# More buffers for the last stage of a one-layer hybrid encoder: eight row tiles, four raw weight tiles, another order in the first MLP chunk

## The chip, the cores and the metric

The kernel runs on one core of one Trainium2 chip. A core has a matrix engine (TensorE, PE in the profile, with its weight loads shown apart as PEld), a vector engine (VectorE, DVE), a scalar engine (ScalarE, ACT), a general engine (GpSimd, POOL), and an engine that here only issues transfers (SyncE, SP). Each engine works through its own instructions in a fixed order and waits on semaphores for the others. The on-chip memory SBUF has 128 partitions; the matrix engine adds up its products in PSUM. The metric is the device time of one execution in microseconds (us), the median of several runs.

## The reference, cut to what matters

The program computes one step of a layer on 2048 prompt rows and 32 sample rows, each 1024 wide, in float32:

```python
qa, ka, va, qb, kb, vb = split_proj(rmsnorm(hp, g_attn), w_in)
oa = diff_attn_prompt(qa, ka, va, t5_table, lam)      # group A
ob = band_attn_prompt(qb, kb, vb, band_table)         # group B
hp = hp + merge(oa, ob, subln_g, out_norm_b, w_out, lam_init)   # concat @ w_out
# ffn_ple:
c = rmsnorm(h, g_mlp)
h = h + jnp.square(jax.nn.relu(c @ w_up)) @ w_down    # 1024 -> 4096 -> 1024
h = h + jax.nn.sigmoid(h @ w_ple_gate) * (p @ w_ple_proj)
y = rmsnorm(h, g_final)
```

The attention outputs are normalised, joined and projected by w_out; then come the MLP, the gate and the final norm. The attention takes most of the program's text and is not touched.

## The kernel before, in words

**Blocks.** The 2080 rows are four blocks of columns (the data lie transposed, features on the partitions): blocks 0 to 2 have 512 columns, block 3 has 544 and is multiplied as two halves of 272. A row of 128 features of one block is one small tile, 128 x 512 or 128 x 544.

**Three products for one.** Every operand is split into a high part, which the matrix engine takes at full speed, and a low part, the rest. `mm3` (L186 to L192) issues hi x hi (L190), hi x lo (L191) and lo x hi (L192) for each of the terms; 24 matmuls make one product of 1024 terms. `split` makes the parts: the high part on ACT (L169), the low part on POOL in pieces of 256 columns at most (L164 for weights, L154 for rows) or on DVE (L175).

**Weights.** `wunit` (L177) brings one unit of 512 KB: a load into a raw tile `wr`, of which there are two, then wh on ACT and wl in four pieces on POOL; wh and wl have three tiles each. A raw tile is free once both parts have been made.

**Small tiles.** One ring of four tiles with the tag "tmp" is shared by five users: `raw_o` loads a row of the attention output (oraw), `outproj` loads the residual row it adds to (hd) and keeps its square (tmp), `cnorm` loads a row of h to be normalised (tmp), and `mlp_up` keeps the relu of a product (relu).

**Order.** The program is written as Python generators that are woven by hand; a list scheduler of the framework then fixes, before the run, the order of each engine's instructions from its own model of durations and of which tiles are free. So the number of tiles changes not only what must wait but also the order. All transfers are issued by SP (L145) in one order: a load whose tile isn't free holds up all those behind it. Where a pool of tiles is opened over the space of an older one, a new tile waits until the old one that lies there was last read.

**The last stage** begins where the pools wk4, fk4, md, acth and hh are opened (about L1225). Blocks 0 and 1 have been through the MLP by then, and gate(1) and final(1) are just ending. What follows:

- `outproj(2)`: for each of eight output rows d, one weight unit, 24 matmuls, the sum with hd on DVE (L860), the square on ACT, its sum on POOL (sqacc), and the store of hd to hS. It is woven with `oload(3)`, which loads the eight rows k of block 3's attention output (oraw), scales four of them (L835, DVE) and splits them (oact).
- `outproj(3)`, the same for block 3, 48 matmuls of 272 columns for each d.
- `gate(0)`: eight weight units of w_ple_gate; the low and high parts of h are hL and hH; sigmoid and sums are sig and sm on ACT, POOL and DVE (L1015 to L1034), and the result goes into h on POOL.
- `cnorm(2)` and `cnorm(3)`: for each of eight rows a load of tmp from hS, a scaling (L881, DVE), and the split into cH (ACT) and cL (POOL for even rows, DVE for odd ones). The parts of block 3 lie where gate(0) has hH and hL, so they wait for its last matmul.
- `final(0)`: transposes (yp), the final norm (yn) and the stores to y_prompt.
- `mlp` on blocks 2 and 3: 16 chunks of two weight units f0, f1; in each, `mlp_up` makes the products (ups) of both units with both blocks, relu, square (L936, L937) and the split into uh and ul; `mlp_down` of the chunk before adds its products (dps) to h (L971, DVE).
- gate(2), gate(3) and their finals end the program.

In `mlp_up` the loop over f stands outside, the loop over the blocks inside; the first products are f0 x block 2, f0 x block 3, f1 x block 2, f1 x block 3.

Of the kernel before, what the change touches and what calls it, by code (L numbers as in the profile page):

```python
# [12 lines left out]
F32 = mybir.dt.float32  # L13
F32R = mybir.dt.float32r
AF = mybir.ActivationFunctionType
# [4 lines left out]
P = 128  # L20
# [13 lines left out]
BLK = 544  # L34
SUBS = {
    0: [(0, 512)],
    1: [(0, 512)],
    2: [(0, 512)],
    3: [(0, 272), (272, 272)],
}  # L40
# [67 lines left out]
class Rings:  # L108
    def __init__(self, *rings):
        self.rings, self.i = rings, 0  # L110
# [23 lines left out]
class Kern:  # L134
    def __init__(self, tc, a):
        self.tc = tc
        self.nc = tc.nc
        self.a = a

    def dma(self, dst, src):  # L140
        if dst.dtype == F32R:
            dst = dst.bitcast(F32)
        if src.dtype == F32R:
            src = src.bitcast(F32)
        self.nc.sync.dma_start(dst, src)  # L145
# [30 lines left out]

    def wunit(self, src, shape, hi_eng="act", lo_eng="pool"):  # L177
        nc = self.nc
        raw = self.wp.tile([P] + shape, F32, tag="wr", bufs=2, name="wr")
        self.dma(raw, src)  # L180
        hi = self.wp.tile([P] + shape, F32R, tag="wh", bufs=3, name="wh")
        lo = self.wp.tile([P] + shape, F32R, tag="wl", bufs=3, name="wl")
        self.split(hi, lo, raw, hi_eng, lo_eng)
        return hi, lo
# [615 lines left out]
                self.dma(self.pS[:, 1, k, t0 : t0 + n], lo[:, :n])  # L800

    def raw_o(self, wk, k, t0, n):
        t = wk.tile([P, BLK], F32, tag="tmp", bufs=4, name="oraw")[:, :n]
        self.dma(t, self.oT[:, k, t0 : t0 + n])
        return t

# [34 lines left out]
    def outproj(self, b, wk, oact, ps, acc):  # L841
        nc, a = self.nc, self.a
        n, t0 = BN[b], 512 * b
        W = a["w_out"][0]
        sq = wk.tile([P, BLK], F32, tag="acc", bufs=2, name="sqacc2")[:, :n]
        acc.append(sq)
        for d in range(8):
            wh, wl = self.wunit(W[:, P * d : P * d + P].rearrange("(k p) c -> p k c", p=P), [8, P])
            h = wk.tile([P, BLK], F32, tag="tmp", bufs=4, name="hd")[:, :n]
            self.dma(h, self.xT[:, d, t0 : t0 + n])  # L850
            for s0, sn in SUBS[b]:
                p = ps.tile([P, 512], F32, tag="mm", name="ops")[:, :sn]
                self.mm3(
                    p,
                    [
                        (wh[:, k], wl[:, k], oact[0][k][:, s0 : s0 + sn], oact[1][k][:, s0 : s0 + sn])
                        for k in range(8)
                    ],
                )
                nc.vector.tensor_tensor(h[:, s0 : s0 + sn], h[:, s0 : s0 + sn], p, op=ALU.add)  # L860
            if d == 0:
                nc.scalar.activation(sq, h, AF.Square)
            else:
                tmp = wk.tile([P, BLK], F32, tag="tmp", bufs=4, name="tmp")[:, :n]
                nc.scalar.activation(tmp, h, AF.Square)
                self.pool_tt(sq, sq, tmp, ALU.add)
            self.dma(self.hS[:, d, t0 : t0 + n], h)
            yield

    def cnorm(self, b, wk, act, out):  # L870
        nc = self.nc
        n, t0 = BN[b], 512 * b
        cH = act.tile([P, 8, act.aw], F32R, tag="act", name="cH")
        cL = act.tile([P, 8, act.aw], F32R, tag="act", name="cL")
        out[b] = (cH, cL)
        r = wk.tile([P, BLK], F32, tag="r", bufs=2, name="rl")[:, :n]
        self.dma(r, self.rS[:, t0 : t0 + n])
        for k in range(8):
            tmp = wk.tile([P, BLK], F32, tag="tmp", bufs=4, name="tmp")[:, :n]
            self.dma(tmp, self.hS[:, k, t0 : t0 + n])  # L880
            nc.vector.scalar_tensor_tensor(  # L881
                tmp, tmp, self.g_mlp[:, k : k + 1], r, op0=ALU.mult, op1=ALU.mult
            )
            self.split(cH[:, k, :n], cL[:, k, :n], tmp, "act", "dve" if k % 2 else "pool")
            yield
# [31 lines left out]
    def mlp_up(self, ch, nf, blocks, st, wk, up, mm):  # L917
        nc = self.nc
        Wu = self.a["w_up"][0]
        us = {}  # L920
        for f in range(nf):
            ft = nf * ch + f
            wh, wl = self.wunit(Wu[:, P * ft : P * ft + P].rearrange("(k p) c -> p k c", p=P), [8, P])
            for b in blocks:
                h, cH, cL = st[b]
                uh = up.tile([P, up.aw], F32R, tag="u", name="uh")
                ul = up.tile([P, up.aw], F32R, tag="u", name="ul")
                us[f, b] = (uh, ul)
                for s0, sn in SUBS[b]:
                    ps = mm.tile([P, 512], F32, tag="mm", name="ups")[:, :sn]  # L930
                    self.mm3(
                        ps,
                        [(wh[:, k], wl[:, k], cH[:, k, s0 : s0 + sn], cL[:, k, s0 : s0 + sn]) for k in range(8)],
                    )
                    r = wk.tile([P, BLK], F32, tag="tmp", bufs=4, name="relu")[:, :sn]
                    nc.scalar.activation(r, ps, AF.Relu)  # L936
                    nc.scalar.activation(r, r, AF.Square)  # L937
                    self.split(uh[:, s0 : s0 + sn], ul[:, s0 : s0 + sn], r, "act", "pool")
        return us

    def mlp_down(self, ch, nf, blocks, us, st, wk, mm):
# [154 lines left out]
    def run(self):  # L1096
        tc, nc, a = self.tc, self.nc, self.a
        with ExitStack() as top:

            def opened(stack, name, bufs, space=None, side="left"):  # L1100
                kw = {} if space is None else {"space": space}
                return stack.enter_context(
                    tc.tile_pool(name=name, bufs=bufs, side=side, reuse_waits="tile", **kw)
                )
# [2 lines left out]
            cp = opened(top, "cp", 1)  # L1107
            self.dp = opened(top, "dp", 1, bass.MemoryType.DRAM)
            self.wp = opened(top, "wp", 3)
            mm = opened(top, "mm", MM, PSUM)  # L1110
            tp = mm
            psx = ExitStack()
# [16 lines left out]
            with ExitStack() as x:  # L1129
                wk = opened(x, "setup", 1, side="right")  # L1130
# [5 lines left out]
            with ExitStack() as x:  # L1136
                pool = opened(x, "a0", 1, side="right")
# [42 lines left out]
            with ExitStack() as x:  # L1180
                pool = opened(x, "a1", 1, side="right")
                for js in JA1:
                    self.attn_a(js, pool, ps_s, ps_t, ps_o)
            wk = opened(sq_, "wk", 1)
            fk = opened(sq_, "fk", 1)
            self.gfin(fk)
            acc, cn, st = {}, {}, {}
# [12 lines left out]
            up = Sized(opened(top, "uh", 16, side="right"), BLK)  # L1200
# [3 lines left out]
            def hload(pool, w, b):  # L1204
                h = pool.tile([P, 8, w], F32, tag="h", name="h")
                self.dma(h[:, :, : BN[b]], self.hS[:, :, 512 * b : 512 * b + BN[b]])
                return h

            for b in HALVES[0]:
# [4 lines left out]
                h = hload(hq, 512, b)  # L1214
# [10 lines left out]
            psx.close()  # L1225
            wk = opened(top, "wk4", 1)
            fk = opened(top, "fk4", 1)
            self.gfin(fk)
            md = opened(top, "md", 8 - MM, PSUM, "right")
            act = Sized(opened(top, "acth", 4), BLK, True)  # L1230
# [6 lines left out]
            h = hload(hh, BLK, 0)  # L1237
# [6 lines left out]
            f = self.final(0, h, up, fk, mm)  # L1244
            st = {b: (hload(hh, BLK, b),) + cn[b] for b in HALVES[1]}
# [6 lines left out]
            f = self.final(2, st[2][0], up, fk, mm)  # L1252
# [4 lines left out]
            f = self.final(3, st[3][0], up, fk, mm, md)  # L1257
# [48 lines left out]
```

## Time and profile before

| what | us |
|---|---|
| median of three runs | 3277.6 (3271.13 to 3279.51) |
| profiled execution, its own time | 3282.74 |
| its span, first to last instruction | 3281.0 |
| PE busy in the span | 3096.6 |
| the last stage's beginning, 2180 to 2460: PE busy | 250.61 of 280 |
| the long MLP, 2460 to 3200: PE busy | 740.00 of 740 |
| the end, 3200 to 3281: PE busy | 67.17 of 81 |

The mean granted clock of PE in the profile is 0.974 of full speed. A row of the timeline gives the start, the duration of the group, the engine, the line, the operation, output and inputs with their shapes, the number of instructions, and in brackets the idle time ahead of it and what ended it. A row of the waits gives the engine and line that waited, the one that it waited for, the total, the number of times and the longest. In a chain of waits each piece is what the next one was waiting for. PE's matmuls overlap: the distance of two starts, not the duration shown, is what one costs.

### The profile page before, as it was taken

The page shows a single profiled execution, that of the slowest core. Times are in us where ns is not written, and L with a number is a line of the kernel's source. Part 1 is how long each engine was busy: PE and PEld are TensorE (multiplying, and loading weights), DVE is VectorE, ACT ScalarE, POOL GpSimd, SP SyncE. Part 2 cuts the span into 40 slices and gives each one's busy share as a digit, 9 for nine tenths or more (in the row PEclk, how much of TensorE's full clock was granted, in tenths as well). Part 3 has the DMA queues.
Part 4 walks back from the last instruction along what each step waited for, and adds up shares of the span by engine and source line. Part 5 has one row for each costly group of instructions (what it writes and reads, how often), then busy time and mean ns, then how long its engine had stood idle before and what let it go on. Part 6 is the DMA issues. An engine that isn't in the chain of part 4 may idle for free.

```text
span 3281.0 us, 51609 instructions
## 1 busy us (share of the span) xinstructions
PE 3096.6 (94%) x17881; PEld 2713.4 (83%) x17881; DVE 1562.2 (48%) x3952; ACT 1696.1 (52%) x3717; POOL 1711.0 (52%) x2515
## 2 busy tenths in 40 slices
PE   6998999899989999999999999998989999999998
PEld 6877788899877888778788877877779999999988
DVE  5116786444455544566655655735442232223235
ACT  4226676666656766666665656744442222222245
POOL 5436776433335544656654644676954333333377
PEclk9998999999999999999999999999989999999999
DMA  7488886876778654545655355357531111111123
GB/s 230 169 258 241 226 246 199 230 225 199 221 210 240 166 140 120 159 137 152 195 136 142 109 139 139 111 159 227 164 102 49 46 46 50 45 48 46 46 91 106
DMA packets 519085, 489.03 MB, mean 149 GB/s; under 512 B 37884, under 2 KB 414016, under 8 KB 518824
## 3 DMA queue, kind: packets, MB, share of 16 engines
q1 hardware_dynamic: 518824, 485.73, 50.8%
q8 instruction: 142, 2.33, 0.3%
q14 instruction: 119, 0.97, 0.1%
HBM read 379.06 MB, written 110.49 MB: 149 GB/s over the span
## 4 chain that ended last, share of the span: by engine, by line
PE 54%; DMA 5%; DVE 4%; POOL 2%; ACT 1%; issue 1%; SPq 0%; DVEq 0%; POOLq 0%; ACTq 0%
PE dps L190 7%; PE ups L191 7%; PE ups L190 7%; PE ups L192 7%; PE dps L192 7%; PE dps L191 7%; PE s L567 2%; PE gps L190 1%; PE gps L191 1%; DMA ka<-kS 1%; PE gps L192 1%; PE tpp L639 1%; POOL wl L164 1%; DMA wr<-w_up 1%; PE ob L766 1%
## 5 line engine op out<-in xcount | busy, mean ns | idle before, releaser
L164 POOL TENSOR_TENSOR wl<-wr,wh 128x256 fp32r<-128x256 f32 x936 | 690.9, 770 | 501.1 <-ACT wh L169 473.0
L971 DVE TENSOR_TENSOR h<-h,dps 128x512 f32<-128x512 f32 (+1 forms) x640 | 373.1, 585 | 597.5 <-PE dps L192 584.9
L169 ACT ACTIVATE wh<-wr 128x1024 fp32r<-128x1024 f32 x338 | 356.9, 1056 | 581.0 <-PE dps L191 285.7
L154 POOL TENSOR_TENSOR wl<-wr,wh 128x256 fp32r<-128x256 f32 x416 | 305.0, 764 | 407.0 <-ACT wh L169 403.7
L190 PE MATMUL dps<-uh,wh 128*128 128x512 f32 (+1 forms) x1280 | 458.6, 358 | 10.1 <-DVE h L971 5.5
L190 PE MATMUL ups<-cH,wh 128*128 128x512 f32 (+1 forms) x1280 | 453.3, 354 | 9.9 <-ACT relu L936 5.0
L191 PE MATMUL ups<-cL,wh 128*128 128x512 f32 (+1 forms) x1280 | 452.9, 354 | 4.1 <-DVE cL L175 3.6
L192 PE MATMUL ups<-cH,wl 128*128 128x512 f32 (+1 forms) x1280 | 453.2, 354 | 0.0
L191 PE MATMUL dps<-ul,wh 128*128 128x512 f32 (+1 forms) x1280 | 451.0, 353 | 0.0
L192 PE MATMUL dps<-uh,wl 128*128 128x512 f32 (+1 forms) x1280 | 450.9, 353 | 0.0
L154 POOL TENSOR_TENSOR ul<-relu,uh 128x136 fp32r<-128x136 f32 (+1 forms) x320 | 201.7, 652 | 167.7 <-ACT uh L169 166.4
L190 PEld LDWEIGHTS ups<-cH,wh 128*128 128x128 f32 x1280 | 242.8, 190 | 42.3 <-ACT relu L936 5.3
L190 PEld LDWEIGHTS dps<-uh,wh 128*128 128x128 f32 x1280 | 242.5, 189 | 42.4 <-DVE h L971 9.0
L191 PEld LDWEIGHTS ups<-cL,wh 128*128 128x128 f32 x1280 | 243.3, 190 | 36.0 <-DVE cL L175 3.8
L192 PEld LDWEIGHTS dps<-uh,wl 128*128 128x128 f32 x1280 | 242.0, 189 | 33.7
L192 PEld LDWEIGHTS ups<-cH,wl 128*128 128x128 f32 x1280 | 243.1, 190 | 30.1
L191 PEld LDWEIGHTS dps<-ul,wh 128*128 128x128 f32 x1280 | 242.2, 189 | 26.2
L190 PE MATMUL qps<-aH,wh 128*128 128x512 f32 (+1 forms) x640 | 231.3, 361 | 8.6 <-ACT kr L432 3.4
L191 PE MATMUL qps<-aL,wh 128*128 128x512 f32 (+1 forms) x640 | 229.6, 359 | 0.0
L192 PE MATMUL qps<-aH,wl 128*128 128x512 f32 (+1 forms) x640 | 228.9, 358 | 0.0
L567 PE MATMUL s<-ka,q 128*128 128x256 f32 (+4 forms) x784 | 190.4, 347 | 26.6 <-DMA ka<-kS 10.9
L581 ACT ACTIVATE e<-s,nm 128x512 f32<-128x512 f32 (+3 forms) x256 | 155.1, 611 | 68.7 <-DVE nm L573 46.0
(218 smaller groups left out, 7118.3 us busy)
## 6 DMA issues: line engine op xcount, KB each, us to landing
wr<-w_up SPq DMA_DIRECT2D x96, 512.0 KB, 4.2
wr<-w_down SPq DMA_DIRECT2D x96, 512.0 KB, 3.7
wr<-w_in SPq DMA_DIRECT2D x74, 512.0 KB, 5.2
q<-qS SPq DMA_DIRECT2D x256, 128.0 KB, 4.2
v<-vSa SPq DMA_DIRECT2D x64, 512.0 KB, 4.0
ka<-kS SPq DMA_DIRECT2D x32, 512.0 KB, 7.7
wr<-w_out SPq DMA_DIRECT2D x32, 512.0 KB, 5.4
wr<-w_ple_gate SPq DMA_DIRECT2D x32, 512.0 KB, 4.3
```

Of the source, the lines that this page charges most:

```text
L154: nc.gpsimd.tensor_tensor(out[:, sl], a[:, sl], b[:, sl], op=op)
L164: nc.gpsimd.tensor_tensor(out[:, sl], a[:, sl], b[:, sl], op=op)
L169: nc.scalar.activation(hi, raw, AF.Copy)
L190: nc.tensor.matmul(ps, lh, rh, start=start and i == 0, stop=False)
L191: nc.tensor.matmul(ps, lh, rl, start=False, stop=False)
L192: nc.tensor.matmul(ps, ll, rh, start=False, stop=stop and i == n - 1)
L567: nc.tensor.matmul(s, q[:, m, hl, P * qi : P * qi + nr], kt[:, m, k0 : k0 + n], start=hl == 0, stop=hl == 1)
L581: nc.scalar.activation(dst, src, AF.Exp, bias=nmx, accum_out=z[:nr, m, bi : bi + 1])
L639: nc.tensor.transpose(tp[:kn, x, :nr], w[:nr, P * i : P * i + kn], self.ident[:nr, :nr])
L766: nc.tensor.matmul(o[:, qa:qb], vt, pt[:kn, i - kfirst, qa:qb], start=x == 0 and y == 0, stop=x == len(order) - 1 and y == 1,)
L971: nc.vector.tensor_tensor(hv, hv, ps, op=ALU.add)
```

## The change: two rings made larger, one loop turned for one chunk, less scratch

- From the last stage on the ring "tmp" has eight tiles and not four (`self.nt`), for all its five users.
- From there on raw weight tiles come in turn from the old ring of two and from a new ring of two in the pool wk4 (`Rings`, a class that is in the kernel already, takes the next ring at each call).
- In the first chunk of each MLP the order of the products is all weight units for one block, then all for the next. It differs from the old order only where there are two blocks, in the last stage. Both weight units of the chunk are then used before block 3 is.
- The scratch that is set aside for descriptors is 1024 bytes. The added tiles need, in each partition, 4 x 544 x 4 = 8704 bytes and 2 x 4096 = 8192 bytes.

No operation is added or removed, and no byte is moved more.

```diff
--- before.py
+++ after.py
@@ -136,6 +136,7 @@
         self.tc = tc
         self.nc = tc.nc
         self.a = a
+        self.nt = 4
 
     def dma(self, dst, src):
         if dst.dtype == F32R:
@@ -176,7 +177,7 @@
 
     def wunit(self, src, shape, hi_eng="act", lo_eng="pool"):
         nc = self.nc
-        raw = self.wp.tile([P] + shape, F32, tag="wr", bufs=2, name="wr")
+        raw = self.rawp.tile([P] + shape, F32, bufs=2, name="wr")
         self.dma(raw, src)
         hi = self.wp.tile([P] + shape, F32R, tag="wh", bufs=3, name="wh")
         lo = self.wp.tile([P] + shape, F32R, tag="wl", bufs=3, name="wl")
@@ -800,7 +801,7 @@
                 self.dma(self.pS[:, 1, k, t0 : t0 + n], lo[:, :n])
 
     def raw_o(self, wk, k, t0, n):
-        t = wk.tile([P, BLK], F32, tag="tmp", bufs=4, name="oraw")[:, :n]
+        t = wk.tile([P, BLK], F32, tag="tmp", bufs=self.nt, name="oraw")[:, :n]
         self.dma(t, self.oT[:, k, t0 : t0 + n])
         return t
 
@@ -846,7 +847,7 @@
         acc.append(sq)
         for d in range(8):
             wh, wl = self.wunit(W[:, P * d : P * d + P].rearrange("(k p) c -> p k c", p=P), [8, P])
-            h = wk.tile([P, BLK], F32, tag="tmp", bufs=4, name="hd")[:, :n]
+            h = wk.tile([P, BLK], F32, tag="tmp", bufs=self.nt, name="hd")[:, :n]
             self.dma(h, self.xT[:, d, t0 : t0 + n])
             for s0, sn in SUBS[b]:
                 p = ps.tile([P, 512], F32, tag="mm", name="ops")[:, :sn]
@@ -861,7 +862,7 @@
             if d == 0:
                 nc.scalar.activation(sq, h, AF.Square)
             else:
-                tmp = wk.tile([P, BLK], F32, tag="tmp", bufs=4, name="tmp")[:, :n]
+                tmp = wk.tile([P, BLK], F32, tag="tmp", bufs=self.nt, name="tmp")[:, :n]
                 nc.scalar.activation(tmp, h, AF.Square)
                 self.pool_tt(sq, sq, tmp, ALU.add)
             self.dma(self.hS[:, d, t0 : t0 + n], h)
@@ -876,7 +877,7 @@
         r = wk.tile([P, BLK], F32, tag="r", bufs=2, name="rl")[:, :n]
         self.dma(r, self.rS[:, t0 : t0 + n])
         for k in range(8):
-            tmp = wk.tile([P, BLK], F32, tag="tmp", bufs=4, name="tmp")[:, :n]
+            tmp = wk.tile([P, BLK], F32, tag="tmp", bufs=self.nt, name="tmp")[:, :n]
             self.dma(tmp, self.hS[:, k, t0 : t0 + n])
             nc.vector.scalar_tensor_tensor(
                 tmp, tmp, self.g_mlp[:, k : k + 1], r, op0=ALU.mult, op1=ALU.mult
@@ -917,25 +918,29 @@
     def mlp_up(self, ch, nf, blocks, st, wk, up, mm):
         nc = self.nc
         Wu = self.a["w_up"][0]
-        us = {}
-        for f in range(nf):
+        us, w = {}, {}
+        order = [(f, b) for f in range(nf) for b in blocks]
+        if ch == 0:
+            order = [(f, b) for b in blocks for f in range(nf)]
+        for f, b in order:
             ft = nf * ch + f
-            wh, wl = self.wunit(Wu[:, P * ft : P * ft + P].rearrange("(k p) c -> p k c", p=P), [8, P])
-            for b in blocks:
-                h, cH, cL = st[b]
-                uh = up.tile([P, up.aw], F32R, tag="u", name="uh")
-                ul = up.tile([P, up.aw], F32R, tag="u", name="ul")
-                us[f, b] = (uh, ul)
-                for s0, sn in SUBS[b]:
-                    ps = mm.tile([P, 512], F32, tag="mm", name="ups")[:, :sn]
-                    self.mm3(
-                        ps,
-                        [(wh[:, k], wl[:, k], cH[:, k, s0 : s0 + sn], cL[:, k, s0 : s0 + sn]) for k in range(8)],
-                    )
-                    r = wk.tile([P, BLK], F32, tag="tmp", bufs=4, name="relu")[:, :sn]
-                    nc.scalar.activation(r, ps, AF.Relu)
-                    nc.scalar.activation(r, r, AF.Square)
-                    self.split(uh[:, s0 : s0 + sn], ul[:, s0 : s0 + sn], r, "act", "pool")
+            if f not in w:
+                w[f] = self.wunit(Wu[:, P * ft : P * ft + P].rearrange("(k p) c -> p k c", p=P), [8, P])
+            wh, wl = w[f]
+            h, cH, cL = st[b]
+            uh = up.tile([P, up.aw], F32R, tag="u", name="uh")
+            ul = up.tile([P, up.aw], F32R, tag="u", name="ul")
+            us[f, b] = (uh, ul)
+            for s0, sn in SUBS[b]:
+                ps = mm.tile([P, 512], F32, tag="mm", name="ups")[:, :sn]
+                self.mm3(
+                    ps,
+                    [(wh[:, k], wl[:, k], cH[:, k, s0 : s0 + sn], cL[:, k, s0 : s0 + sn]) for k in range(8)],
+                )
+                r = wk.tile([P, BLK], F32, tag="tmp", bufs=self.nt, name="relu")[:, :sn]
+                nc.scalar.activation(r, ps, AF.Relu)
+                nc.scalar.activation(r, r, AF.Square)
+                self.split(uh[:, s0 : s0 + sn], ul[:, s0 : s0 + sn], r, "act", "pool")
         return us
 
     def mlp_down(self, ch, nf, blocks, us, st, wk, mm):
@@ -1107,6 +1112,7 @@
             cp = opened(top, "cp", 1)
             self.dp = opened(top, "dp", 1, bass.MemoryType.DRAM)
             self.wp = opened(top, "wp", 3)
+            self.rawp = Rings((self.wp, "wr"))
             mm = opened(top, "mm", MM, PSUM)
             tp = mm
             psx = ExitStack()
@@ -1225,6 +1231,8 @@
             psx.close()
             wk = opened(top, "wk4", 1)
             fk = opened(top, "fk4", 1)
+            self.nt = 8
+            self.rawp = Rings((self.wp, "wr"), (wk, "wr"))
             self.gfin(fk)
             md = opened(top, "md", 8 - MM, PSUM, "right")
             act = Sized(opened(top, "acth", 4), BLK, True)
@@ -1282,7 +1290,7 @@
     for n in ("cache_a_k", "cache_a_v", "cache_b_k", "cache_b_v"):
         arrays[n] = arrays[n].reshape(PAST, 512)
     arrays["onehot_a"], arrays["onehot_b"] = onehots()
-    nc = bacc.Bacc("TRN2", target_bir_lowering=False, num_devices=1)
+    nc = bacc.Bacc("TRN2", target_bir_lowering=False, num_devices=1, dynamic_dma_scratch_size=1024)
     a = {}
     for n, v in arrays.items():
         a[n] = nc.dram_tensor(n, v.shape, mybir.dt.from_np(v.dtype), kind="ExternalInput").ap()
```

## The prediction

> **What bounds the kernel now.** I read the page's busy shares first, then busy time and clock by stretch, then what TensorE (PE) waited for in the last stage, and then the timelines around those waits.
>
> ```profile
> PE 3096.6 (94%) x17881; PEld 2713.4 (83%) x17881; DVE 1562.2 (48%) x3952; ACT 1696.1 (52%) x3717; POOL 1711.0 (52%) x2515
> ```
> ```profile
> 2200.00:2220.00 20.00, 20.00 (x98) 16.43 (x97) 12.84 (x19) 9.96 (x20) 16.89 (x21) 1.00 0.93 303
> ...
> 2240.00:2260.00 20.00, 15.37 (x74) 12.93 (x73) 14.47 (x18) 11.59 (x19) 18.21 (x20) 0.83 0.63 202
> 2260.00:2280.00 20.00, 15.32 (x99) 15.01 (x98) 6.48 (x10) 4.94 (x8) 7.39 (x11) 0.83 0.72 236
> ...
> 2340.00:2352.00 12.00, 5.95 (x16) 4.29 (x15) 9.91 (x12) 6.57 (x10) 12.00 (x14) 0.72 0.54 175
> ...
> 2382.00:2404.00 22.00, 11.24 (x52) 10.27 (x50) 12.65 (x11) 6.00 (x10) 15.01 (x21) 0.61 0.32 99
> ...
> 2460.00:3268.00 808.00, 806.65 (x5021) 732.17 (x5019) 244.18 (x467) 262.40 (x482) 374.92 (x592) 1.00 0.18 56
> ```
>
> The columns after the length are busy time of PE, its weight loads, DVE, ACT and POOL, then granted clock, DMA share and GB/s. PE bounds the whole; the long MLP (2460 to 3268) loses 1.35 us in 808, so prefetching its weights deeper can win no more than that. In the part the change touches, PE is short in three places only: **A**, the start of outproj(3), idle 9.3 us of 40; **B**, inside gate(0), 6.1 of 12; **C**, the first MLP chunk, 10.8 of 22. Each also shows a clock under 1. The waits, from 2180 to 2460:
>
> ```profile
> PE gps L190 <- ACT wh L169: 6.1, 1, 6.1
> ...
> PE ops L190 <- DVE hd L860: 4.7, 1, 4.7
> ...
> PE ops L190 <- ACT oact L169: 1.6, 1, 1.6
> PE ops L191 <- DVE oact L175: 1.6, 1, 1.6
> PE ops L192 <- POOL wl L164: 1.4, 1, 1.4
> ```
>
> **The change part by part.** It adds and removes no operation: the same matmuls, splits and bytes, in the order that the scheduler now fixes. In that order, which is fixed before the run, the engines' lists are the same up to the last stage, but for the load of gf, which goes earlier.
>
> *C, the first MLP chunk.*
>
> ```profile
> 2375.63 2.31 ACT L169 ACTIVATE cH<-tmp 128x544 fp32r<-128x544 f32 x4 [3.23 <-PE gps L191]
> 2382.67 0.29 PE L190 MATMUL ups<-cH,wh 128*128 128x272 f32 x1
> ...
> 2386.90 0.59 PE L191 MATMUL ups<-cL,wh 128*128 128x272 f32 x1 [3.57 <-DVE cL L175]
> ...
> 2391.31 0.59 PE L190 MATMUL ups<-cH,wh 128*128 128x272 f32 x1 [2.23 <-ACT cH L169]
> 2396.86 0.59 PE L190 MATMUL ups<-cH,wh 128*128 128x272 f32 x1 [4.96 <-ACT relu L936]
> ...
> 2402.70 0.40 PE L191 MATMUL ups<-cL,wh 128*128 128x272 f32 x1
> ...
> 2403.06 0.29 PE L190 MATMUL ups<-cH,wh 128*128 128x272 f32 x1
> ```
> ```profile
> L175 DVE TENSOR_TENSOR cL<-tmp,cH x6: 714/1085/9979, 2346.9 to 2396.0; 128x544 fp32r<-128x544 f32 x4, 128x512 fp32r<-128x512 f32 x2
> ```
> ```profile
> 2377.45 3.31 POOL L154 TENSOR_TENSOR cL<-tmp,cH 128x181 fp32r<-128x181 f32 x6
> 2380.67 5.59 POOL L164 TENSOR_TENSOR wl<-wr,wh 128x256 fp32r<-128x256 f32 x8
> ```
> ```profile
> 2387.78 5.43 DMA tmp<-hS
> ```
>
> After the 24 matmuls on block 2, PE comes to block 3 at 2382.67 and gets the last at 2396.86. Two things hold them: a cL of DVE that takes 9.98 us (the fastest 0.71) while POOL ran its two rows back to back, 2377.45 to 2386.26, and the second four tmp tiles, whose loads, under way at 2387.78, wait for the tiles that this same cL holds. The idle time is 3.57 + 2.23 + 4.96 = 10.8 us. Behind the last wait the 272-wide matmuls start 0.226 us apart until 2402.70 and 0.126 after that, so 5.8 us hold 26 matmuls that need 3.3: 2.5 us lost, and about 0.8 behind the first wait (8 matmuls). C costs 14.1 us.
>
> With eight tiles all eight loads go ahead, and DVE's eight L881 stand in one run before the rest of the gate; with the new order, block 3 is asked for after 48 matmuls of block 2 (48 x 0.234 = 11.2 us) and not after 24. The matmuls of block 2 end at 2382.67 in the trace and so begin at 2377.05; block 3 is asked for at 2388.3 at the earliest. The price: the second weight unit is needed at once, and on POOL its wl stands behind all of block 3's cL pieces. Twelve cL pieces of 0.55 (six took 3.31) put the first wl piece, 0.70, at 2377.45 + 6.6 + 0.7 = 2384.75, while PE needs it at 2382.7: 2.1 us idle, and about 2.3 us of slow clock, by what B shows below. DVE's held cL would come free at POOL's end of run, 2377.45 + 12 x 0.55 + 8 x 0.70 = 2389.7, two more cL at 1.0 make 2391.7, and PE with its 4.4 us delay asks for block 3 at 2392.7: covered. C falls from 14.1 to 4.4, gain 9.7; the ends are 5 (another 5 us of block 3 late) and 14 (all of it gone). Its cover is thin: without the 24 matmuls between, the held cL shows again.
>
> *A, the start of outproj(3).*
>
> ```profile
> 2246.94 3.46 DVE hL L175 x3
> ...
> 2258.06 0.69 DVE hd L860
> ...
> 2259.86 5.66 DMA oraw<-oT
> ...
> 2266.36 0.70 DVE hd L860
> 2267.10 0.60 PE ops L190
> ...
> 2273.14 0.23 PE ops L192
> ```
>
> The tiles k of block 3 (oraw) and the sums d of block 2 (hd) share the ring. The link is: hd d, its store, the next oraw load behind it on SP's queue, L835, and the next hd behind that on DVE: 2258.06 to 2266.36, 8.3 us. With eight tiles no tile is missing, but SP's order still sends each load after the store of an earlier hd, so links remain; DVE now takes hd d4 before the three hL and oact, 3.5 us earlier, and PE has 38 matmuls of the first product in a row that it had not. So I let the first three waits go by two thirds (4.6 x 2/3 = 3.1) and about 1 us of the slow clock with them, and leave the 4.7 of the chain: gain 4. Ends: 0, and all of A, 9.3 + 5 (2267.10 to 2273.14 is the same slow spacing, 2.7 us, and the first waits have about as much).
>
> *B, gate(0), fourth unit.*
>
> ```profile
> 2345.49 1.05 ACT wh L169
> ...
> 2347.37 0.43 PE gps L191
> ...
> 2351.64 0.34 PE pps L191
> 2352.43 0.23 PE pps L191
> ```
>
> wh waited on ACT behind cH, behind DVE's L881 that had no tiles sooner. It comes 3 to 4 us earlier now. But POOL is busy for 12.00 of these 12 us, and the fourth wl comes from it: gain 1 (0 to 4). The slow matmuls after it, 12 of them at 0.427 and not 0.234, are the 2.3 us used above.
>
> *A new wait at the start of the stage (A1).*
>
> ```profile
> 2181.63 0.37 SPq L145 DMA_DIRECT2D wr<-w_out  x1
> ...
> 2196.77 0.33 SPq L145 DMA_DIRECT2D gf<-g_final  x1
> ```
> ```profile
> h<-hS SPq DMA_DIRECT2D x1, 2048.0 KB, 11.4
> ...
> gf<-g_final SPq DMA_DIRECT2D x1, 512.0 KB, 6.7
> ```
> ```profile
> 2198.19 4.65 POOL L164 TENSOR_TENSOR wl<-wr,wh 128x256 fp32r<-128x256 f32 x4
> ...
> 2208.80 1.43 POOL L154 TENSOR_TENSOR h<-h,sig 128x256 f32<-128x256 f32 x2
> ```
> ```profile
> 2200.73 0.39 PE L190 MATMUL ops<-ou,wh 128*128 128x512 f32 x1
> ```
>
> The two added raw tiles lie in the stage's own pool, over space that gate(1) still reads. The second weight unit of outproj(2) falls on one of them: its load stands on SP behind the wait for gate(1)'s last matmul, about 2198, and no longer at 2181.63. It stands where gf's 512 KB stood, which landed after 6.7 us, so at about 2204.7; wh adds 1.05. POOL now does gate(1)'s last sig and h before that wl, h ending near 2206.9 (2208.80 + 1.43 = 2210.2 before; no wl of 2 to 4 us stands ahead of it now). PE reaches that unit's low part near 2208.4; from 2200.73 it has 16 ops matmuls (3.7) and 12 short yp (1.5), so 2.5 us are idle. With part of a slow stretch (2.3 in B, taken as 1.5) the loss is 4. Ends: 0, and 8.2 (a landing after 11.4 us, as the 2 MB load of h beside it, gives 5.7 idle and 2.5 slow).
>
> [...] In the trace 3.57 us of idle time was enough, and the whole of A, where no single wait before 2258 was over 1.6 us, has a clock of 0.83, so I keep the slow stretches.
>
> *Scratch and the rest.* The program issues its loads from SP (518824 packets on the hardware queue); a smaller scratch is only room, priced 0. The end of the kernel has a few transposes exchanged: 0, plus or minus 1 us.
>
> Sum: 9.7 + 4 + 1 - 4 = 10.7 us. The profiled execution took 3282.74 us (span 3281.0), so 3272.0; it is 5.1 us above the median of 3277.6 of the three runs shown, which gives 3266.9, about 3267.
>
> **The rivals.**
>
> *R1, it ends slower.* Not block 3 but f1's weights are what PE waits for. On ACT wh of f1 stands behind all eight cH of block 3, on POOL its wl behind twelve pieces. If tmp's second four still arrive near 2393, wh f1 comes at 2397 and wl's first piece at 2398: 15.3 us from 2382.7, with the slow stretch 17.6, against 14.1. C loses 3.5; with the other terms (+4 + 1 - 4) the time is 3280. It decides from the point where the last cH comes later than about 2393 instead of 2381. For it: ACT's order is in line. Against it: eight tiles are free when the loads are issued.
>
> *R2, POOL shuts DVE out for longer.* [...] As a mechanism of this kernel: POOL's run grows from 8.8 to 12.2 us, and if it begins later, or each piece takes 1.16 (4.65 / 4) as at 2198, DVE's cL comes at 2396 and block 3 is 5 us late: C gains 4.7, time 3272.
>
> *R3, A1 does not show and A mostly goes.* If the weights of that second unit land while POOL is still at the gate, and the freed ring unties the links, A gains 10, A1 costs 1: 10 + 10 + 1 - 1 = 20, 3258.
>
> *R4, it does nothing measurable.* A loses what A1 pushes into it, and C is R2's: under 5 us, 3274.
>
> **How the numbers follow.** Forecast 0.48, R1 0.14, R2 0.13, R3 0.14, R4 0.11. 0.3% is 9.8 us, about what a measurement of this kernel can tell from no change: below 3267.8 is faster. The forecast with its errors lies there about six times in ten, R3 always, R2 and R4 one in four, R1 never: 0.29 + 0.14 + 0.06, about 0.5. Slower than 3287.4 needs R1 and the upper end of A1 at once, or something that I don't see: 0.12. The range, 3253 to 3283, reaches from R3 with B's upper end to R1 with 3 us more.
>
> **What would show it.** C: PE asks for block 3 about 2389, with no wait above 2 us on cL, cH or relu; a wait of some 2 us for f1's wl; tmp loads in a run of eight. A: fewer waits near the first oact, one of 4 to 5 us for hd left. A1: a wait for the wh or wl of outproj(2)'s second unit where before PE was busy 20.00 of 20. I am wrong if PE waits for f1's wh on ACT (R1), if cL still holds it (R2), or if the MLP after 2460 is no longer full.

## The result, and the profile after

The changed kernel takes 3264.07 us (median of 20 runs, 3251.01 to 3275.71) against 3279.03 of the kernel before beside it (20 runs, 3270.78 to 3292.62). The ratio is 0.9956, 95% interval 0.9946 to 0.9967: 0.44% faster, 11 to 18 us. The forecast was 3267, a gain of 10.7 us.

Busy shares of the changed kernel, from its page, and busy time and clock by stretch (the columns are those of the prediction):

```profile
span 3268.2 us, 51485 instructions
...
PE 3084.2 (94%) x17881; PEld 2703.7 (83%) x17881; DVE 1567.8 (48%) x3952; ACT 1694.2 (52%) x3717; POOL 1711.4 (52%) x2515
```
```profile
2460.00:3200.00 740.00, 740.00 (x4519) 667.53 (x4518) 208.17 (x391) 225.11 (x383) 325.16 (x503) 1.00 0.18 53
```
```profile
2200.00:2210.00 10.00, 8.91 (x43) 6.60 (x42) 8.66 (x13) 7.84 (x16) 7.13 (x9) 1.00 1.04 340
...
2250.00:2260.00 10.00, 6.59 (x29) 6.27 (x29) 7.27 (x8) 2.90 (x4) 10.00 (x12) 0.66 0.63 220
...
2330.00:2340.00 10.00, 5.57 (x24) 4.14 (x23) 10.00 (x13) 4.91 (x8) 10.00 (x11) 0.91 0.70 205
...
2370.00:2380.00 10.00, 4.91 (x21) 3.55 (x20) 10.00 (x1) 6.07 (x10) 10.00 (x19) 0.95 0.04 14
2380.00:2390.00 10.00, 6.62 (x26) 6.21 (x27) 5.74 (x6) 2.27 (x4) 6.21 (x10) 0.53 0.34 107
```

The long MLP is as full as before. The three places are still there, each smaller or of another kind, and a small one has come in at 2200. What PE waited for in the beginning of the last stage:

```profile
PE ups L191 <- ACT relu L941: 8.5, 1, 8.5
PE pps L191 <- DVE sm L1021: 5.6, 1, 5.6
PE ops L192 <- DVE oact L176: 3.2, 1, 3.2
...
PE ops L191 <- ACT oact L170: 1.1, 2, 0.7
PE ops L192 <- DVE ou L176: 1.1, 2, 0.8
```

(Lines of the changed kernel are one to five higher: L170 is the high part on ACT, L155 and L165 the low parts on POOL, L176 the low part on DVE, L191 to L193 the three products, L882 the scaling in cnorm, L941 the relu.) The waits for hd and for the gate's wh are gone; one of 8.5 us for relu and one of 5.6 for sm are new.

Single executions differ before they come to this stage: in these profiles the first product with ou starts between 2180.87 us (relu_own_cl3) and 2200.22 (cl3_swap). So I compare stretches inside it, read off PE's timeline as distances of starts: outproj(2) from the first product with ou to the first with oact; outproj(3) from there to its last; the gate from there to the first ups; the MLP from there to the last dps. All runs of this study are in the table, with one profile each; the ratio is to the kernel before in the same session. The scratch alone (scr_only) has the order of the kernel before on every engine, so it also shows how far two profiles of one order differ: 0.3 to 2 us per stretch.

| run | outproj(2) | outproj(3) | gate(0) | MLP | sum | ratio, 95% |
|---|---|---|---|---|---|---|
| before | 50.5 | 64.5 | 65.5 | 764.8 | 945.3 | 1 |
| scr_only | 49.9 | 62.5 | 65.8 | 764.2 | 942.4 | 1.0005, 0.9992 to 1.0017 |
| changed | 51.2 | 56.4 | 64.2 | 760.6 | 932.4 | 0.9956, 0.9946 to 0.9967 |
| nt_only | 49.3 | 57.3 | 64.8 | 757.8 | 929.2 | 0.9965, 0.9952 to 0.9977 |
| raw_only | 53.6 | 61.0 | 63.6 | 763.8 | 941.9 | 0.9970, 0.9955 to 0.9985 |
| ord_only | 50.1 | 63.0 | 64.9 | 760.1 | 938.1 | 0.9986, 0.9974 to 0.9998 |
| no_ord | 52.1 | 56.5 | 63.9 | 759.3 | 931.8 | 0.9966, 0.9952 to 0.9979 |
| relu_own | 51.8 | 53.0 | 63.0 | 760.3 | 928.0 | 0.9965, 0.9953 to 0.9978 |
| cl3_dve | 51.2 | 56.6 | 64.2 | 749.3 | 921.3 | 0.9941, 0.9927 to 0.9955 |
| cl3_dve_wl | 53.2 | 55.8 | 65.3 | 750.6 | 924.9 | 0.9957, 0.9942 to 0.9973 |
| before_cl3 | 50.3 | 62.7 | 65.4 | 755.3 | 933.7 | 0.9969, 0.9958 to 0.9981 |
| cl3_swap | 51.2 | 56.8 | 64.1 | 760.5 | 932.6 | 0.9957, 0.9941 to 0.9972 |
| cl3_wide | 51.4 | 56.3 | 64.1 | 755.9 | 927.7 | 0.9956, 0.9941 to 0.9971 |
| relu_own_cl3 | 51.3 | 53.3 | 63.1 | 749.3 | 916.9 | 0.9911, 0.9894 to 0.9928 |

By this table the change won 6 to 8 us in outproj(3), 4 in the MLP's first chunk and 1 to 2 in the gate, and lost about 1 in outproj(2): 10 to 13 us in all.

### The profile page after: what moved, and what is told of

It reads as the page before. It is cut to its first block, busy times and chain, and to the rows that moved or that the text cites. A ratio compares the mean times of both kernels' runs of the same rounds, so it can differ in the third digit from the quotient of the medians.

```text
span 3268.2 us, 51485 instructions
## 1 busy us (share of the span) xinstructions
PE 3084.2 (94%) x17881; PEld 2703.7 (83%) x17881; DVE 1567.8 (48%) x3952; ACT 1694.2 (52%) x3717; POOL 1711.4 (52%) x2515
## 4 chain that ended last, share of the span: by engine, by line
PE 55%; DVE 5%; DMA 3%; ACT 2%; POOL 1%; issue 1%; SPq 0%; DVEq 0%; POOLq 0%; ACTq 0%
PE dps L191 7%; PE ups L191 7%; PE ups L192 7%; PE ups L193 7%; PE dps L193 7%; PE dps L192 7%; PE s L568 2%; PE gps L191 2%; PE gps L192 2%; PE gps L193 1%; DMA ka<-kS 1%; PE tpp L640 1%; PE ob L767 1%; DMA wr<-w_up 1%; PE o L655 1%
## 5 line engine op out<-in xcount | busy, mean ns | idle before, releaser
L165 POOL TENSOR_TENSOR wl<-wr,wh 128x256 fp32r<-128x256 f32 x936 | 690.3, 769 | 484.4 <-ACT wh L170 457.1
L170 ACT ACTIVATE wh<-wr 128x1024 fp32r<-128x1024 f32 x338 | 356.8, 1056 | 578.6 <-PE dps L192 264.5
L155 POOL TENSOR_TENSOR wl<-wr,wh 128x256 fp32r<-128x256 f32 x416 | 306.2, 767 | 407.2 <-ACT wh L170 400.2
L191 PE MATMUL dps<-uh,wh 128*128 128x512 f32 (+1 forms) x1280 | 457.0, 357 | 11.8 <-DVE h L976 7.1
L191 PE MATMUL ups<-cH,wh 128*128 128x512 f32 (+1 forms) x1280 | 452.9, 354 | 10.8 <-ACT relu L941 8.5
L193 PE MATMUL ups<-cH,wl 128*128 128x512 f32 (+1 forms) x1280 | 453.1, 354 | 0.0
L193 PE MATMUL dps<-uh,wl 128*128 128x512 f32 (+1 forms) x1280 | 450.5, 352 | 0.0
L155 POOL TENSOR_TENSOR ul<-relu,uh 128x136 fp32r<-128x136 f32 (+1 forms) x320 | 201.4, 651 | 163.1 <-ACT uh L170 161.2
L191 PEld LDWEIGHTS dps<-uh,wh 128*128 128x128 f32 x1280 | 242.0, 189 | 44.3 <-DVE h L976 10.4
L191 PEld LDWEIGHTS ups<-cH,wh 128*128 128x128 f32 x1280 | 242.4, 190 | 43.3 <-ACT relu L941 9.3
L193 PEld LDWEIGHTS dps<-uh,wl 128*128 128x128 f32 x1280 | 241.3, 189 | 33.0
L193 PEld LDWEIGHTS ups<-cH,wl 128*128 128x128 f32 x1280 | 242.8, 190 | 30.2
L191 PE MATMUL qps<-aH,wh 128*128 128x512 f32 (+1 forms) x640 | 229.8, 359 | 10.7 <-ACT kr L433 3.7
L193 PE MATMUL qps<-aH,wl 128*128 128x512 f32 (+1 forms) x640 | 228.2, 357 | 0.0
L582 ACT ACTIVATE e<-s,nm 128x512 f32<-128x512 f32 (+3 forms) x256 | 155.1, 611 | 64.9 <-DVE nm L574 42.7
```

The costliest lines, as they stand in the source:

```text
L155: nc.gpsimd.tensor_tensor(out[:, sl], a[:, sl], b[:, sl], op=op)
L165: nc.gpsimd.tensor_tensor(out[:, sl], a[:, sl], b[:, sl], op=op)
L170: nc.scalar.activation(hi, raw, AF.Copy)
L191: nc.tensor.matmul(ps, lh, rh, start=start and i == 0, stop=False)
L193: nc.tensor.matmul(ps, ll, rh, start=False, stop=stop and i == n - 1)
L582: nc.scalar.activation(dst, src, AF.Exp, bias=nmx, accum_out=z[:nr, m, bi : bi + 1])
```

## The experiments

### Each part alone

nt_only: the changed kernel without these lines.

```diff
-            self.rawp = Rings((self.wp, "wr"), (wk, "wr"))
-        if ch == 0:
-            order = [(f, b) for b in blocks for f in range(nf)]
```

> Eight small tiles alone (two raw weight tiles, the old order in the first chunk, 1024 bytes of scratch). Theory T: the 8 us that the start of outproj(3) (A) gained come from the small tiles, so A gains 6 to 9 us here too; the first MLP chunk (C) stays within 2 us of before, because block 3 is still asked for after 24 matmuls and DVE's held cL still gives back the tile late. Time 6 to 9 us under the kernel before, ratio 0.997 to 0.998. Rival U: A's gain comes from the raw tiles, which let SP send transfers that waited behind a weight load; then A keeps its waits here and the time is within 3 us of before.

Theory T holds for outproj(3): 57.3 against 62.5 to 64.5. The MLP gained 6 to 7 us too, which T did not expect, and the whole is 11 us faster (0.9965), more than T's 6 to 9.

raw_only: without `self.nt = 8` and without the order.

> Four raw weight tiles alone. Theory T: A and C keep their waits, the start of the stage loses about 1 us to the later load of the second weight unit: 0 to 2 us over the kernel before, ratio 1.000 to 1.001. Rival U: A loses 6 to 9 us of its waits, the time is 6 to 9 us under the kernel before.

Neither holds in full. Waits of the run with four raw tiles alone:

```profile
PE ops L191 <- DVE hd L861: 3.3, 1, 3.3
...
PE ops L191 <- ACT wh L170: 1.3, 1, 1.3
```

The wait for hd stays in outproj(3), as T has it, and the second unit's wh is now waited for, which makes outproj(2) 3 to 4 us longer. But the ratio, 0.9970, says 5 to 15 us faster over twelve runs, and in this profile, which is the longest of its runs, the stage is only 0.5 to 3.4 us shorter. What the raw tiles are worth alone stays open.

ord_only: without `self.nt = 8` and the second ring of raw tiles.

> The order of the first chunk alone, with four small and two raw tiles. Theory T: only C can change; block 3's second four rows still come near 2393, but up to 24 matmuls (5.6 us) of block 2 lie ahead of them now, less 2 us of waiting for the second unit's wl: 2 to 5 us under the kernel before. Rival R1 of the prediction: the second unit's weights stand behind block 3's cH, C loses up to 3 us: over the kernel before.

T holds: the MLP is 4 to 5 us shorter, the rest is as before within the 2 us by which two profiles differ. Of the waits of this run one is of a kind that the kernel before did not have so long:

```profile
PE ups L191 <- ACT relu L941: 9.2, 1, 9.2
...
PE ops L191 <- DVE hd L861: 4.5, 2, 4.3
```

scr_only: `dynamic_dma_scratch_size=1024` alone.

> The scratch of 1024 bytes alone; the order of every engine is that of the kernel before. Expected by all theories: no change, 0 plus or minus 2 us, ratio within 0.0007 of 1. If the scratch bears on how transfers are issued, every stage with a DMA share over 0.6 moves and the time changes by over 10 us.

No difference, as forecast.

no_ord: the changed kernel without the order.

> The change without the order of the first chunk: eight small tiles, four raw tiles. Theory T (parts add up as their stretches did alone): as the eight small tiles alone plus the 0 to 3 us that the raw tiles cost outproj(2): C (from the first ups to the last dps) near 758 us, the whole within 3 us of the changed kernel. Rival S: the order is needed for C also with eight tiles; then C is 764 or more and the kernel 4 us over the changed one.

The MLP stretch is 759.3, and the time is not told apart from the changed kernel's. So the order, worth 4 us with four tiles, is worth nothing with eight: T is nearer than S. The two do not add up in the first chunk.

### What holds the first chunk

The changed kernel there: PE, DVE and ACT by the timeline.

```profile
2374.51 0.40 PE L192 MATMUL ups<-cL,wh 128*128 128x512 f32 x1
2383.38 0.60 PE L191 MATMUL ups<-cH,wh 128*128 128x272 f32 x1 [8.47 <-ACT relu L941]
```
```profile
2369.40 13.87 DVE L176 TENSOR_TENSOR cL<-tmp,cH 128x544 fp32r<-128x544 f32 x2 [4.79 <-ACT cH L170]
```
```profile
2382.73 0.60 ACT L941 ACTIVATE relu<-ups 128x512 f32<-128x512 f32 x1 [6.66 <-DVE cL L176]
```

The chain of waits shows the first of DVE's two cL alone, and POOL follows:

```profile
2369.40 13.25 DVE cL L176
2382.73 0.60 ACT relu L941
```
```profile
2370.15 6.46 POOL L155 TENSOR_TENSOR cL<-tmp,cH 128x181 fp32r<-128x181 f32 x12
2376.57 5.49 POOL L165 TENSOR_TENSOR wl<-wr,wh 128x256 fp32r<-128x256 f32 x8
```

Three links make one wait. The first cL of DVE, which began 0.75 us before POOL's first cL while POOL was at other work without a gap, has a row of 13.24 us that lasts until 2382.64; POOL's run, with the 20 operations shown at its end, ends at 2382.06, 0.58 us earlier. The second cL takes the usual 0.71. By the profile relu is released by the end of that first cL: block 3's rows hold all eight tmp tiles, and relu needs one. And relu must empty a PSUM tile of the first product before PE may begin the product that stands next in its order. That order is not the one written in the loop: after 24 matmuls of the first product and two of the second, the list puts 19 of block 3, and only then the other 22.

relu_own is meant to separate the ring from the cL: six tiles for rows and two for relu.

```diff
-                r = wk.tile([P, BLK], F32, tag="tmp", bufs=self.nt, name="relu")[:, :sn]
+                r = wk.tile([P, BLK], F32, tag="rel", bufs=2, name="relu")[:, :sn]
-            self.nt = 8
+            self.nt = 6
```

(Before the last stage the relu tile stays in its old ring, here as in relu_own_cl3.)

> The changed kernel with the same eight tiles shared out: six for the rows, two for relu alone. Theory L (DVE's cL is shut out while POOL runs without a gap; the relu only passes the wait on through the ring): the relu wait of 8.5 us goes, but PE then waits 5 us or more for cL of DVE, and DVE's long cL stays over 8 us: 0 to 4 us under the changed kernel. Rival Q (the ring is the cause: relu wants the tile, all else would be ready): no wait over 2 us is left in C and it is 6 to 9 us shorter than in the changed kernel, 752 to 755 us.

```profile
2359.53 12.77 DVE L176 TENSOR_TENSOR cL<-tmp,cH 128x544 fp32r<-128x544 f32 x2 [4.36 <-ACT cH L170]
```
```profile
2376.40 0.60 PE L191 MATMUL ups<-cH,wh 128*128 128x272 f32 x1 [7.01 <-ACT relu L941]
```

Q's forecast fails: with a ring of its own relu is almost as late (7.0 us), and the MLP is 760.3. So does L's, that the wait for relu goes and one for cL takes over. On ACT relu stands behind a cH whose row DVE scales only after the long cL; with six tiles that row is loaded only when the long cL (2359.53 to 2371.66) has freed a tile, and scaled at 2374.39. So the ring still has a part in this run, and it is the next runs that separate the two. The long cL is there, 12.13 us. The ratio, 0.9965, is not told apart from the changed kernel's. The gain of outproj(3), 53.0 against 56.4, I had not foreseen.

cl3_dve takes POOL's share of block 3's low parts away.

```diff
-            self.split(cH[:, k, :n], cL[:, k, :n], tmp, "act", "dve" if k % 2 else "pool")
+            self.split(cH[:, k, :n], cL[:, k, :n], tmp, "act", "dve" if k % 2 or b == 3 else "pool")
```

> The changed kernel with all eight low parts of block 3's rows on DVE (before: four on POOL). Theory L: POOL's unbroken run is then the eight wl pieces, 5.5 us; the longest cL of DVE is 4 to 7 us, ends within 1.5 us of the end of that run, and the rest follow at 0.7: the wait in C falls from 8.5 to about 3. Rival M (the long row is a wait for something else than POOL, booked as duration): the longest cL stays near 13 us, or is under 1.3 us.

```profile
2361.36 3.74 DVE L176 TENSOR_TENSOR cL<-tmp,cH 128x544 fp32r<-128x544 f32 x4 [4.34 <-PE pps L193]
2365.63 3.71 DVE L176 TENSOR_TENSOR cL<-tmp,cH 128x544 fp32r<-128x544 f32 x4
```
```profile
2366.68 6.75 POOL L165 TENSOR_TENSOR wl<-wr,wh 128x256 fp32r<-128x256 f32 x8 [4.06 <-ACT wh L170]
```
```profile
engine op xcount: duration ns min/median/max, first and last start us, forms
L176 DVE TENSOR_TENSOR cL<-tmp,cH x8: 707/712/1839, 2361.4 to 2368.1; 128x544 fp32r<-128x544 f32 x8
```

DVE does eight in about half the time that two had taken, its longest is 1.84 us, and POOL's eight wl pieces take 6.75 us beside them, not 5.49. The wait in C is gone, with relu still in the ring of eight, so Q falls here; the MLP is 11.3 us shorter than in the changed kernel. PE's list changed too (44 matmuls of block 2 ahead of block 3, not 26), so not all of this need be the cL; before_cl3 below has no such change. L's sign is right, its size wrong: it expected a cL of 4 to 7 us, since POOL still has a run of eight pieces. The first cL is again the longest, and it again ends 0.58 us after POOL's run, but that run (sig) ends at 2362.62, since POOL must then wait for ACT's wh. DVE was already at work when POOL began the eight pieces, and neither was held for long: DVE's second four take 3.71 us, POOL's eight the 6.75.

cl3_dve_wl takes away that run as well: the low parts of the two weight units on DVE.

```diff
-                w[f] = self.wunit(..., [8, P])
+                w[f] = self.wunit(..., [8, P], "act", "dve" if len(blocks) == 2 and ft in (1, 2) else "pool")
```

> As the run before, and the low parts of the two weight units that POOL made beside it (f1 of the first chunk, f0 of the second) on DVE too, so that POOL has no run there. Theory L: no cL of DVE over 1.3 us, eight of them in 6 us, block 3 is ready before PE has done the 48 matmuls of block 2: no wait over 2 us in C, C 6 to 9 us shorter than in the changed kernel, 752 to 755 us. Rival M: a long cL is there still.

```profile
2363.36 2.63 DVE L176 TENSOR_TENSOR cL<-tmp,cH 128x544 fp32r<-128x544 f32 x4 [5.28 <-PE pps L193]
2366.51 2.62 DVE L176 TENSOR_TENSOR cL<-tmp,cH 128x544 fp32r<-128x544 f32 x4
```

With POOL silent one cL costs 0.66 us (four in 2.63), and no wait over 1 us is left in C. L holds, with more gain than forecast (10 us against 6 to 9). The MLP, 750.6, is not better than in cl3_dve, where C has no wait to lose.

before_cl3 makes that one edit in the kernel before.

> The kernel before with all eight low parts of block 3's rows on DVE and nothing else changed: four small tiles, two raw tiles, the old order. Theory L (the held cL is what made C long, the four tiles only pass it on): no cL of DVE over 2 us, the second four loads go before 2382 and not near 2387, C 4 to 9 us shorter than before (764.8), 756 to 761. Rival N (four tiles are too few by themselves): the loads still come late, the waits for cH and relu stay, C within 3 us of 764.8.

```profile
2376.53 4.85 DVE L175 TENSOR_TENSOR cL<-tmp,cH 128x544 fp32r<-128x544 f32 x4 [3.79 <-ACT cH L169]
2386.82 4.76 DVE L175 TENSOR_TENSOR cL<-tmp,cH 128x544 fp32r<-128x544 f32 x4
```
```profile
L175 DVE TENSOR_TENSOR cL<-tmp,cH x10: 711/1246/2403, 2347.6 to 2390.3; 128x544 fp32r<-128x544 f32 x8, 128x512 fp32r<-128x512 f32 x2
```
```profile
PE ups L191 <- DVE cL L175: 3.4, 1, 3.4
```
```profile
2380.23 3.66 DMA tmp<-hS
```
```profile
2379.65 9.01 POOL L164 TENSOR_TENSOR wl<-wr,wh 128x256 fp32r<-128x256 f32 x8 [1.30 <-ACT wh L169]
```

L holds in the main: the second four loads are under way at 2380.23 and not at 2387.78, and the MLP stretch falls by 9.5 us, a little more than forecast, with four tiles, two raw tiles and the old order. PE takes its products in the order of the kernel before (24 matmuls of block 2, 48 of block 3, 24, 48), so the gain is not one of order. L's "no cL over 2 us" fails: the first is 2.40 us, ending 0.58 us after POOL's run at that point, and a wait of 3.4 us for cL is left of the 10.8. In the first chunk this one word is worth twice what the whole change won there.

cl3_swap and cl3_wide ask when POOL shuts DVE out: the even rows on DVE and the odd on POOL; and POOL's pieces 272 wide and not 181.

```diff
# cl3_swap
-"dve" if k % 2 else "pool"
+"dve" if (k + (b == 3)) % 2 else "pool"
# cl3_wide, in pool_tt for cL of block 3 only
-            m = -(-n // PW)
+            m = m or -(-n // PW)     # m = 2
```

> The changed kernel with the even rows' cL of block 3 on DVE and the odd ones on POOL, the other way round, so that DVE is first to begin. Theory F (who streams first keeps the other from more than one turn): DVE does k0 and goes on with k2, no cL over 2 us, C 749 to 753. Rival G (any run of POOL without a gap shuts DVE out from its second operation on, whoever began): a cL of 10 us or more, ending 1.2 us after POOL's run, C within 2 us of the changed kernel, 758 to 763.

> The changed kernel with POOL's cL of block 3 in two pieces of 272 columns and not three of 181 or 182. Rival G: the run of POOL is as long (8 x 0.75 + 5.5), one cL of DVE takes 10 us or more and ends 1.2 us after it. Rival P (the odd width makes the conflict): no cL over 2 us, C 749 to 753.

DVE and POOL of the first, then of the second; the last line is the first cL of cl3_swap alone, from the chain of waits:

```profile
2372.57 14.54 DVE L176 TENSOR_TENSOR cL<-tmp,cH 128x544 fp32r<-128x544 f32 x2 [4.17 <-PE pps L193]
```
```profile
2373.95 6.50 POOL L155 TENSOR_TENSOR cL<-tmp,cH 128x181 fp32r<-128x181 f32 x12
2380.39 5.51 POOL L165 TENSOR_TENSOR wl<-wr,wh 128x256 fp32r<-128x256 f32 x8
```
```profile
2371.28 13.38 DVE L176 TENSOR_TENSOR cL<-tmp,cH 128x544 fp32r<-128x544 f32 x2 [4.75 <-ACT cH L170]
```
```profile
2372.03 5.93 POOL L155 TENSOR_TENSOR cL<-tmp,cH 128x272 fp32r<-128x272 f32 x8
2377.86 5.58 POOL L165 TENSOR_TENSOR wl<-wr,wh 128x256 fp32r<-128x256 f32 x8
```
```profile
2372.57 13.92 DVE cL L176
```

The forecasts of F and P fail; the width does not matter here (12.74 us with pieces of 272 columns, 13.24 with 181). In cl3_swap DVE's first cL began 1.4 us before POOL's first cL and was held itself, not the second as G had it. But POOL was then at h and sig and had worked without a gap for 28 us at least (from 2344.11). So the swap did not make DVE the first to begin, and whether that would help is not tested by it. In both runs the long row ends 0.6 us after POOL's run, 2386.48 after 2385.90 and 2384.03 after 2383.44. cl3_wide has an MLP of 755.9 nonetheless, since its list of PE happens to put eight matmuls of the second product, not two, ahead of block 3, and the wait for relu is 4.4 us and not 8.5.

### The version that beats both

relu_own_cl3: six tiles for rows, two for relu, block 3's cL on DVE, the rest as in the change.

> The changed kernel with six small tiles for rows and two for relu, and block 3's cL on DVE: the two edits that each went below the changed kernel. If they add up: outproj(3) about 53 us and C about 750, from the first product of outproj(2) to the last of the MLP 917 to 920, that is 2 to 4 us under the run with cL on DVE alone (921.3); ratio to the kernel before 0.992 to 0.994. If six tiles are too few for C once cL is quick, tmp's last two loads come late, PE waits over 2 us for cL or relu, and it is no better than 921.

Its longest waits in this part of the stage:

```profile
PE gps L191 <- ACT wh L170: 2.4, 2, 2.2
PE ops L192 <- DVE oact L176: 2.0, 2, 1.1
PE pps L191 <- DVE sm L1021: 1.5, 1, 1.5
```

The two edits add up in the stretches: 921.3 + 928.0 - 932.4 = 916.9 by the runs with one each, 916.9 measured. The time is 3250.73 us against 3278.32, ratio 0.9911 (0.9894 to 0.9928), better than the 0.992 to 0.994 expected and than the ratios of the two alone would give; why the whole time gains more is not shown. None of the three places has a wait over 2.2 us.

## Why the prediction was right, and where not

**The whole.** 3264 against 3267, within the range, and the gain of 10.7 us at the lower end of the measured 11 to 18. But the sum was made of four terms (C 9.7, A 4, B 1, A1 minus 4), and three of them were off, with errors that cancelled: C gave about 6 less, A about 3 more and A1 cost 3 less. That the total came out is luck in part.

**C, the first MLP chunk: 9.7 forecast, about 4 measured.** The step that failed is "block 3 is asked for after 48 matmuls of block 2". The loop is written so, but the scheduler's list asks after 26. The cover of 11.2 us, which the forecast itself called thin, was not there, and DVE's held cL showed. That it would last to the end of POOL's run was in the working, at 2389.7 and two more cL after it; the run became longer as forecast (20 operations for 14) and the row with it, 13.24 us for 9.98. PE's 8.47 us of waiting and the 19 slow matmuls behind it (0.227 us apart, not 0.126) are most of the C that is left. The other step missed is the ring: relu is the fifth user of tmp, and with eight rows of block 3 in eight tiles it must wait for one. So rival R2 was the nearest, with C's gain at 4.7, though by way of relu and PSUM and not by block 3's operands. R1 did not come: wh of f1 was done by 2375.03 (2373.03 + 2.00), and PE did not wait for it. The forecast wait of 2.1 us for f1's wl is hidden here behind the one for relu; in cl3_wide it shows, 1.9 us.

**A, the start of outproj(3): 4 forecast, 6 to 8 measured.** That the tiles pay here is shown by nt_only against raw_only and ord_only. The step that was mis-sized is "leave the 4.7 of the chain". A transfer of 5 us and a row that PE needs after it are still there:

```profile
2260.95 5.06 DMA oraw<-oT
...
2266.04 0.80 DVE oraw L836
...
2267.57 0.77 PE ops L191 x4
```
```profile
2253.05 0.60 PE L192 MATMUL ops<-oact,wh 128*128 128x272 f32 x1 [3.21 <-DVE oact L176]
...
2267.57 0.77 PE L191 MATMUL ops<-oact,wh 128*128 128x272 f32 x4 [0.74 <-ACT oact L170]
```

PE comes to this row at 2267.57 and waits only 0.74 us for it. It has done 94 matmuls of block 3 by then; the kernel before had done 60 at its wait of 4.7 us, which ended at 2267.10, and had another row still to come (scaled by DVE at 2270.59, where the last one here is scaled at 2266.04). So the rows come some 5 us sooner, and in the new list products of the next output rows stand ahead of the wait. One wait of 3.21 us is left, with a clock of 0.66 in its ten us.

**A1, the start of the stage: 4 forecast, about 1 measured.** The wait for the second unit's wh is there with the raw tiles alone (1.3 us, the stretch 3 to 4 us longer). In the whole change PE waits 1.1 us for ou, is busy 8.91 of 10 from 2200, and the clock stays at 1.00. The term that was too big is the idle time with its slow stretch. The load landed at 2204.67, as worked out, and wh was done by 2205.74, but PE came to that unit only at 2206.46, with 24 matmuls of the first behind it; and the short gaps did not lower the clock.

**B, the gate: 1 forecast, 1 to 2 measured.** The wait for wh went, and another came in its place:

```profile
2319.66 7.04 DVE L882 SCALAR_TENSOR_TENSOR tmp<-tmp,g_mlp_s,rl 128x512 f32<-128x512 f32 x6
...
2327.52 2.37 DVE L882 SCALAR_TENSOR_TENSOR tmp<-tmp,g_mlp_s,rl 128x512 f32<-128x512 f32 x2
...
2340.45 0.68 DVE L1021 TENSOR_SCALAR sm<-gps 128x512 f32<-128x512 f32 x1
```
```profile
2341.18 0.79 PE L191 MATMUL pps<-pT,wh 128*128 128x512 f32 x1 [5.61 <-DVE sm L1021]
```

Eight tiles let the scheduler put cnorm's eight scalings, each 1.17 us beside POOL, into DVE's list ahead of the gate's sm, 9.4 of the 21 us for which DVE works without a gap up to there, and PE waits 5.61 us for that. nt_only has the same list, with this sm at 2340.50; there PE waits 4.1 us for wh first and only 0.9 for sm, since its raw tiles are two. With six tiles (relu_own) the wait for sm is 1.6. The forecast named POOL as the limit and did not price DVE's list here.

**Scratch: 0**, as scr_only shows.

**The clock.** The changed kernel's trace has a wait of 3.21 us with slow matmuls behind it (0.227 us apart and not 0.126; clock 0.66 in the ten us from 2250). In the kernel before they stand behind waits of 1.60 and 1.56 us within 4 us: from 2253.43 its matmuls start 0.227 us apart (clock 0.66 in the ten us from 2250). So the slow stretches were rightly kept for C and A; for A1 none came: with gaps of 0.32 and 0.77 us the clock stayed at 1.00 in the ten us from 2200. How short a single wait can be and still have slow matmuls behind it, these runs do not tell.

**The shut-out.** In all ten profiles with a long cL (9.61 to 13.91 us) it is DVE's first of block 3, it began while POOL worked without a gap, POOL starts 14 to 21 more operations while it lasts, and it ends 0.57 to 0.59 us after POOL's next gap begins. Elsewhere the two take turns: in the gate of the changed kernel each scaling takes 1.17 us and each of POOL's cL pieces beside it 1.10 (four in 4.38), and in before_cl3 the second four cL take 1.19 each and the wl pieces 1.13 (eight in 9.01), against 0.66 for a cL with POOL silent (cl3_dve_wl) and 0.69 for a wl piece in the changed kernel while DVE is held (eight in 5.49). In the three runs with block 3's cL on DVE and the weights' wl on POOL (cl3_dve, before_cl3, relu_own_cl3) the first cL is held in the same way, but only for 1.84 to 2.40 us: POOL's gap comes soon. So what the edit does is to give POOL a gap early. What makes the two take turns in one place and not in the other is open, since DVE also took turns with a POOL that had no gap (the scalings above); neither the width of POOL's pieces nor which rows are whose decides it.

## What to carry to other kernels

More buffers also change the order, so read the order that the scheduler makes of them and not the loop: it decided three of the four terms here. A ring that several users share passes a wait from one to another; ask of each user what happens when the others hold all tiles. And when an operation's row is ten times its neighbours', look at what ran unbroken beside it: moving half of a short job off GpSimd won more in the first chunk (9.5 us) than the whole change did there (4).

## What the runs showed of the hardware that I had not expected

A VectorE operation with two inputs in SBUF was held for 13.24 us, until 0.58 us into GpSimd's next gap, though GpSimd started 21 operations in that time and each was over in 0.57 to 0.75 us; in the kernel before it was 14 operations and 9.98 us. With GpSimd silent the same operation took 0.66 us (cl3_dve_wl), with turns taken 1.2 (four in 4.76, before_cl3).
